# When the right factors of a matrix product are split and loaded at changes of stage

## The chip, the cores and the metric

The kernel runs on one core of a Trainium2 chip. The metric is the device time of one execution in microseconds (us); the time before is the median of three executions. A profile of one further execution shows what each engine did: TensorE (PE; its weight loads are shown as PEld), VectorE (DVE), ScalarE (ACT), GpSimd (POOL) and SyncE (SP), and the transfers (DMA) that the queues of SP, POOL and ACT issue.

## The reference

One layer of a decoder trunk over 512 tokens with 2048 channels, all in float32. The normalised input is projected into four token mixers (a gated linear recurrence, causal pooling, a short gated convolution and attention with a forget gate) and four gates per channel. Each mixer's output goes through its own branch product, is multiplied by the sigmoid of its gate, and the four are summed. Then come an output product with a residual, and an MLP of width 8192 with a squared ReLU and a residual. What the change touches is the part from the gates on:

```python
branches = jnp.einsum('bskw,kwd->bskd', ys, w_branch[l])
gates = jax.nn.sigmoid(gate_logits.reshape(b, s, N_BRANCH, d))
merged = jnp.sum(gates * branches, axis=2)
x = x + merged @ w_out[l]
h = rms_norm(x, norm_mlp_g[l]) @ w_mlp_up[l]
x = x + jnp.square(jax.nn.relu(h)) @ w_mlp_down[l]
```

## The kernel before

**Precision.** TensorE multiplies a reduced float32 form (fp32r). Each operand is split into a rounded part (names with h: `uh`, `sh`, `mgh`) and a remainder (l: `ul`, `sl`, `mgl`). ACT casts the rounded part, DVE subtracts it from the source to get the remainder, and `mm3` (L182) does three matmuls: high by high, high by low, low by high.

**Products in blocks.** Gates, MLP up and MLP down (kinds g, u and d) are computed in pairs of 128-row output tiles by a two-by-two block scheme with seven products instead of eight (`run_pair`, L923). The left factors are weights: four quarters of a 128 x 1024 raw tile (`wqg`, `wqu`, `wqd`), loaded by SP into four buffers, of which DVE forms sums (L671, into `z` tiles or in place) before they are split (`Item.cast` on ACT, L713; `Item.sub` on DVE, L719; three buffers each). The right factors are the activations: for each of eight keys a tile of seven blocks of 256 columns (the four blocks of the activation and three sums of them, made by `token_sums`, L852), split into `sh` and `sl`, 1792 columns each. A product of a pair is eight keys by three matmuls, 24 matmuls of 256 columns; a pair is 168. Seven products are evicted from PSUM by ACT copies (L936) and DVE adds (L919).

**Slots.** The split right factors lie in slots (`spools`, nine at most); `slot_of` (L865) says which key lies where. Gates and MLP up use eight fixed keys. In MLP down the keys form a sliding window over 32 tiles taken cyclically: pair n uses keys n to n+7, so from one pair to the next one new factor is needed, n+8, and it goes to a slot that the window has left. The results of MLP up are stored to device memory (`zd`) with their sums, and come back as staged tiles `std`. `bring` (L1229) does that: it issues the load of a key into a staging buffer when called (one buffer, `st1`, in the steady pairs; two at the change of stage), queues the cast `shd` (L884) and the remainder `sld` (L888), and after `sld` starts the next load into the buffer that came free.

**Changes of stage.** The last pair of one stage's products and the first of the next are done as duos (`run_duo`, L943): two pairs together in two parts, the first part with keys 0 to 3, the second with keys 4 to 7, so that some slots come free half a stage early. Between gates and MLP up lies the out stage (L1184): the merged tiles (16 slices of 128 channels, `mgh` and `mgl`) are stored to memory as they are made and loaded back in `load_merged` (L1105) into a pool that takes the place of four slots; the last two slices, 7 and 15, stay on the chip and are split there (L1131, L1132). Its last two output tiles are computed interleaved. The out results make the right factors of MLP up: factors 0 to 3 are split as they come (`in_parts`), 4 to 6 are stored and loaded back, and 7 is split at the end.

**The order of the work.** PE, ACT and DVE run in the order in which the program writes their instructions; POOL's and SP's instructions are ordered by the framework. The program runs through a list of left factors with `step` (L806): step n casts the left factor n+2, evicts the last product (`settle`, over `pending`), makes the sums for n+3 or else takes one task that waits, subtracts for n+2, writes the product's matmuls, and then takes more waiting tasks as long as an estimate of DVE's time (`busy`, advanced by `spend`) is not past an estimate of TensorE's (`clock`, advanced by `mm`). Tasks are put on the waiting list by `wait_for` (L772) with a due time on that clock. `result` (L798) forces those left by an earlier pair when a new result tile is taken, and `flush` all.

**Gates and branches.** The branch products (`bk`) were stored earlier; `next_b` (L1053) loads one back for each gate pair through POOL into a single tile `b`, after the multiply (L1070) that used the last one. **The residual** of MLP down is kept in memory (`x1d`): each pair's result is added to it by an accumulating DMA (`put`, L1298), and for the last eight pairs SP then copies the sum to the output; for the very last pair the residual is loaded, added on DVE and stored.

Of the kernel before, what the change touches and what calls it, by code (L numbers as in the profile page):

```python
# [15 lines left out]
P = 128  # L16
# [82 lines left out]
def body(nc, tc, ctx, dram):  # L99
# [672 lines left out]
    def wait_for(fn, n=0, after=0.0):  # L772

        later.append((clock[0] + after, n, fn, era[0]))

    def pop(task=None):
        task = task or later[0]
        later.remove(task)
        _, n, fn, of = task
# [13 lines left out]
    def flush(until=lambda: False):  # L793
        settle()
        while later and not until():
            pop()
# [9 lines left out]
    def step(products):  # L806
# [5 lines left out]
        settle()  # L812
        if did["sums"] <= n + 3 < len(items) and items[n + 3].sums():
# [51 lines left out]
    def slot_of(key):  # L865
# [27 lines left out]
    def in_parts(key, src, after=0.0):  # L893
        first, second = parts_of(key, src)
        wait_for(first, 0, after)
        wait_for(second, 7 * H, after)
# [26 lines left out]
    def run_pair(phase, out, u):  # L923
# [7 lines left out]
        def products(item):  # L931
            (i,) = item.group
            p = ps[at[i]]
            product(phase, i, item.left, p, i not in (2, 3), True, i in (2, 3))
            if i in (1, 2):
                return [lambda: A.copy(c11, p)]  # L936
            args = {6: (u2, p, c11), 7: (u3, p, u2), 4: (c21, p, u3), 5: (c22, p, u3), 3: (c12, p, u2)}[i]
            return [lambda: add(*args)]
# [121 lines left out]
    def merge(n, g):  # L1060
# [8 lines left out]
        def first():  # L1069
            V.tensor_tensor(out=m if k == 0 else g, in0=g, in1=b, op=ALU.mult)  # L1070
            next_b(n + 1)
# [20 lines left out]
    next_b(0)  # L1092

# [9 lines left out]
    mgpool = []  # L1103

    def load_merged():  # L1105
        closed(*(spools[j] for j in (3, 2, 1, 0)))
        mgpool.append(opened("merged", "right"))
        stage["a"] = mgpool[0][1]
        BUFS["a"] = 28
# [18 lines left out]
    for e in range(2):  # L1128
# [4 lines left out]
        mg[7 + 8 * e] = (hi, lo)  # L1133
# [11 lines left out]
    def residual(n, ps):  # L1145
# [5 lines left out]
        def first():  # L1151
# [3 lines left out]
            wait_for(scaled, S)  # L1155
            wait_for(square)

        if e == 0:
            factors[j] = wide(f"x2_{j}", *((st1, "st1", 1) if j % 2 else (opool, "o", 1)))
        o = factors[j]  # L1160
# [7 lines left out]
        def scaled():  # L1168
            V.scalar_tensor_tensor(
                out=o[:, e * S : (e + 1) * S], in0=r, scalar=pc("g_mlp", n), in1=p, op0=ALU.mult, op1=ALU.mult,  # L1170
            )
            if e:
                wait_for(sums, 4 * 300)

        def sums():
            token_sums(o)
            if j < 4:
                in_parts(("u", j), o)
            elif j < 7:
                G.dma_start(zd["u"][j], o)  # L1180
# [3 lines left out]
    for j in range(7):  # L1184
        for n in (j, j + 8):
            ps = bank(f"pw{n}")
            before = None
            for h in range(2):

                def products(item):  # L1190
# [5 lines left out]
                    for k in ks:  # L1196
                        wk = [t[:, k % 8 * P : (k % 8 + 1) * P] for t in ws[k // 8]]
                        mm3(ps, wk, mg[k], k == 0, h == 1 and k == ks[-1])
# [5 lines left out]
    for h in range(2):  # L1204

        def products(item):
            other = items[taken[0]].left
            for k in range(8):
                for (n, ps), w in zip(last.items(), (item.left, other)):
                    wk = [t[:, k * P : (k + 1) * P] for t in w]  # L1210
                    mm3(ps, wk, mg[8 * h + k], h == 0 and k == 0, h == 1 and k == 7)
            return []

        step(products)
        step(lambda item: [r for n, ps in last.items() for r in residual(n, ps)] if h else [])
    flush()
    up_scale = t512("g", "ups")
    A.copy(up_scale, ip)
    closed(mgpool[0])
    for j in range(4):  # L1220
        spools[j] = opened(f"t{j}", "right")
# [183 lines left out]
```

## Time and profile before

| | |
|---|---|
| median of three runs | 2849.2 us (2846.93 to 2855.21) |
| the profiled execution | 2849.29 us, of which the span from the first to the last instruction is 2847.5 |
| PE busy | 2738.3 us (96%), 19808 matmuls |
| DVE busy | 2167.8 us (76%) |
| ACT busy | 1230.2 us (43%) |
| memory | 151 GB/s on the mean |

Stages by the first matmul of each: gates until about 1270, out until 1457, MLP up until 2112 (its first duo until 1516, its last duo from 2072), MLP down to the end (its first duo until 2189). In the lines of the profile, out<-in names a tile and what it is made from; a bracket gives the idle time of the engine ahead of an instruction and what ended it. A row of the windows view gives a stretch, its length, each engine's busy time with its count of instructions, the clock granted to TensorE, the share of the DMA engines and GB/s.

### The profile page before, as it was taken

How to read it: one execution, taken by the hardware profiler on the slowest of the kernel's cores; microseconds unless marked ns; L12 is line 12 of the kernel's file. 1: busy time of each engine (PE TensorE's matmuls, PEld its weight loads, DVE VectorE, ACT ScalarE, POOL GpSimd, SP SyncE). 2: the span in 40 equal slices, each digit the busy share in tenths (PEclk: the TensorE clock that was granted, in tenths of full speed). 3: DMA queues.
4: the chain of work that ended last, by engine and by line, in shares of the span. 5: the costliest groups of instructions: out<-in, count | busy, mean ns of one | idle time of the engine just before them, and what ended most of it. 6: DMA issues, size and time to landing. Idle time of an engine off the chain costs nothing. (4 is left out here: it accounts for less than half of the span.)

```text
span 2847.5 us, 47968 instructions
## 1 busy us (share of the span) xinstructions
PE 2738.3 (96%) x19808; PEld 2550.9 (90%) x19808; DVE 2167.8 (76%) x2662; ACT 1230.2 (43%) x1520; POOL 179.4 (6%) x296
## 2 busy tenths in 40 slices
PE   8999999999999999999989999999977899999999
PEld 7787777789999999997879999999977899999998
DVE  6865654568888888875568988888887677777777
ACT  5443434554444444443233444444444444444443
POOL 3000000000000000021100000000000000000000
PEclk9999999999999999999999999999988999999999
DMA  5232223664444444474544444544444555555565
GB/s 181 85 97 88 78 69 128 201 217 138 147 150 155 142 155 146 145 229 152 166 144 150 160 156 151 163 143 157 162 169 158 154 147 171 172 158 162 173 192 148
DMA packets 143468, 431.31 MB, mean 151 GB/s; under 512 B 16648, under 2 KB 29576, under 8 KB 143248
## 3 DMA queue, kind: packets, MB, share of 16 engines
q1 hardware_dynamic: 101392, 279.19, 30.1%
q0 software_dynamic: 32208, 131.48, 15.6%
q10 hardware_dynamic: 9648, 17.57, 1.7%
q8 instruction: 155, 2.54, 0.4%
q14 instruction: 65, 0.53, 0.1%
HBM read 350.95 MB, written 80.89 MB: 152 GB/s over the span
## 5 line engine op out<-in xcount | busy, mean ns | idle before, releaser
L719 DVE TENSOR_TENSOR uld<-wqd,uhd 128x1024 fp32r<-128x1024 f32 (+3 forms) x136 | 157.2, 1158 | 90.9 <-ACT uhd L713 90.9
L713 ACT CAST uhg<-wqg 128x1024 fp32r<-128x1024 f32 (+1 forms) x136 | 135.5, 999 | 185.3 <-PE pgd L173 96.4
L713 ACT CAST uhu<-wqu 128x1024 fp32r<-128x1024 f32 (+1 forms) x144 | 136.3, 952 | 166.9 <-PE pud L173 88.8
L713 ACT CAST uhd<-wqd 128x1024 fp32r<-128x1024 f32 (+3 forms) x136 | 135.3, 997 | 154.5 <-PE pda L173 72.9
L151 DVE TENSOR_TENSOR wl<-wr,wh 128x1024 fp32r<-128x1024 f32 (+2 forms) x100 | 121.6, 1218 | 89.2 <-ACT wh L150 88.9
L719 DVE TENSOR_TENSOR ulg<-wqg,uhg 128x1024 fp32r<-128x1024 f32 (+1 forms) x136 | 157.1, 1157 | 33.6 <-ACT uhg L713 33.6
L150 ACT CAST wh<-wr 128x1024 fp32r<-128x1024 f32 (+2 forms) x100 | 101.1, 1014 | 159.6 <-PE pb L173 34.1
L719 DVE TENSOR_TENSOR ulu<-wqu,uhu 128x1024 fp32r<-128x1024 f32 (+1 forms) x144 | 157.7, 1100 | 13.4 <-PE pw L173 8.3
L713 ACT CAST uhg<-zg 128x1024 fp32r<-128x1024 f32 (+1 forms) x102 | 102.0, 1000 | 150.0 <-DVE ulg L719 103.3
L713 ACT CAST uhd<-zd 128x1024 fp32r<-128x1024 f32 (+3 forms) x102 | 101.8, 998 | 150.2 <-DVE zd L671 78.0
L173 PE MATMUL pda<-sld,uhd 128*128 128x256 f32 x480 | 138.2, 288 | 27.6 <-DVE sld L888 27.5
L713 ACT CAST uhu<-zu 128x1024 fp32r<-128x1024 f32 (+1 forms) x108 | 103.2, 955 | 125.4 <-DVE ulu L719 77.7
L173 PE MATMUL pdd<-shd,uhd 128*128 128x256 f32 x480 | 137.1, 286 | 3.4 <-DVE y L919 1.9
L173 PE MATMUL pda<-shd,uld 128*128 128x256 f32 x480 | 136.4, 284 | 3.8 <-DVE uld L719 3.6
L173 PE MATMUL pdd<-shd,uld 128*128 128x256 f32 x480 | 136.1, 284 | 3.5 <-DVE uld L719 3.5
L173 PE MATMUL pda<-shd,uhd 128*128 128x256 f32 x480 | 135.6, 283 | 0.4 <-ACT shd L884 0.4
L173 PE MATMUL pdd<-sld,uhd 128*128 128x256 f32 x480 | 135.6, 282 | 0.0
L173 PE MATMUL pdb<-shd,uld 128*128 128x256 f32 x480 | 134.5, 280 | 0.0
L173 PE MATMUL pdb<-sld,uhd 128*128 128x256 f32 x480 | 134.5, 280 | 0.0
L173 PE MATMUL pdb<-shd,uhd 128*128 128x256 f32 x480 | 134.4, 280 | 0.0
L173 PE MATMUL pgd<-shg,ulg 128*128 128x256 f32 x480 | 134.3, 280 | 0.0
L173 PE MATMUL pgb<-shg,ulg 128*128 128x256 f32 x480 | 134.3, 280 | 0.0
(1447 smaller groups left out, 10481.6 us busy)
## 6 DMA issues: line engine op xcount, KB each, us to landing
wqg<-in_w SPq DMA_DIRECT2D x120, 512.0 KB, 3.5
wqu<-in_w SPq DMA_DIRECT2D x112, 512.0 KB, 3.5
wr<-in_w SPq DMA_DIRECT2D x84, 512.0 KB, 3.5
std<-zd POOLq DMA_DIRECT2D x39, 896.0 KB, 6.9
zd<-h POOLq DMA_DIRECT2D x32, 896.0 KB, 4.8
bk<-b ACTq DMA_DIRECT2D x64, 256.0 KB, 2.7
b<-bk POOLq DMA_DIRECT2D x32, 512.0 KB, 4.5
wo<-in_w SPq DMA_DIRECT2D x32, 512.0 KB, 3.5
```

The costliest lines, as they stand in the source:

```text
L150: A.copy(hi, raw)
L151: V.tensor_tensor(out=lo, in0=raw, in1=f(hi), op=ALU.subtract)
L173: T.matmul(out, w, x, start=start, stop=stop, skip_group_check=more)
L713: A.copy(self.hi[:, sl], self.phase.source(i))
L719: V.tensor_tensor(out=lo, in0=self.phase.source(i), in1=f(hi), op=ALU.subtract)
```

## The change

- Waiting tasks can be marked `must`: `step` takes all of them that are due, right after the evictions and ahead of the sums and the subtraction, whatever the estimate of DVE's time; the others are taken as before.
- `bring` goes. `fetch` issues a load, `place_down` queues cast and remainder of a staged factor as `must` and then fetches a named following key into the buffer, and `renew` does this at given times. Around the change from up to down, keys 0 and 1 are loaded two pairs ahead, 0 to 3 are due at 0, 2.5, 11 and 15 from the second part of up's last duo, 4 to 7 at the same times from the start of down's first, 8 and 9 at 1 and 9 from its second part. In a steady pair n, factor n+8 is due 1.4 after the start, and factor n+9 is fetched behind it.
- The merged slices are loaded into the slots' own tiles instead of a pool in their place: six slices of 512 columns at three to a tile, and the seventh in two halves of 256 columns, for each half of the keys. `out_product` runs over these pieces. The last two output tiles are computed one after the other in each half, not interleaved. After the first half, factors 4 and 5 of MLP up are fetched; 6 and 7 are split from the tiles in which they were made.
- The branch tile `b` has two buffers, loaded two gates ahead.
- The last pair's residual is loaded ahead and added to blocks as they come; its output leaves in three stores.

```diff
-    def wait_for(fn, n=0, after=0.0):
-        later.append((clock[0] + after, n, fn, era[0]))
+    def wait_for(fn, n=0, after=0.0, must=False):
+        later.append((clock[0] + after, n, fn, era[0], must))
...
-    def next_task():
-        return next((t for t in later if t[0] <= clock[0]), None)
+    def next_task(must=False):
+        return next((t for t in later if t[0] <= clock[0] and t[4] == must), None)
...
             ensure("cast", n + 2)
             settle()
+        while t := next_task(True):
+            pop(t)
         if did["sums"] <= n + 3 < len(items) and items[n + 3].sums():
...
-        if kind == "u" or j < 8:
-            return (j + 4) % 8
-        return {8: 4, 9: 5, 10: 8}[j] if j < 11 else slot_of((kind, j - 9))
+        if kind == "u":
+            return (4, 5, 6, 7, 3, 2, 0, 1)[j]
+        return {8: 4, 9: 5, 10: 8}[j] if j in (8, 9, 10) else (j + 4) % 8 if j < 8 else slot_of((kind, j - 9))
...
+    def fetch(key, where):
+
+        t = wide(f"st{key[0]}{key[1]}", *where)
+        G.dma_start(t, zd[key[0]][key[1] % UP])
+        return t
...
-            b = wide(f"b{k}_{j}", gpool, "b", 1, 1024)
+            b = wide(f"b{k}_{j}", gpool, "b", 2, 1024)
...
-            next_b(n + 1)
+            next_b(n + 2)
...
-        closed(*(spools[j] for j in (3, 2, 1, 0)))
-        mgpool.append(opened("merged", "right"))
-        for n in (*range(7), *range(8, 15)):
-            mg[n] = [t512("a", f"mg{q}{n}", F32R) for q in "hl"]
-            for q, t in zip("hl", mg[n]):
-                G.dma_start(t, md[q, n])
+        for at, slots in ((0, (2, 3)), (8, (0, 1))):
+            room = [
+                spools[n][1].tile([P, 7 * H], F32R, name=f"mg{q}s{n}", tag=f"s{q}{n}", bufs=1)
+                for n in slots for q in "hl"
+            ]
+            for i in range(6):
+                both = []
+                for q in range(2):
+                    t, c = divmod(2 * i + q, 3)
+                    both.append(room[t][:, c * S : (c + 1) * S])
+                    G.dma_start(both[q], md["hl"[q], at + i])
+                mg[at + i] = [(slice(0, S), both)]
+            mg[at + 6] = []
+            for h in range(2):
+                sl = slice(h * H, (h + 1) * H)
+                both = [room[2 * q + h][:, 3 * S :] for q in range(2)]
+                for q in range(2):
+                    G.dma_start(both[q], md["hl"[q], at + 6][:, sl])
+                mg[at + 6].append((sl, both))
+
+    def out_product(ps, left, k, first, last):
+        wk = [t[:, k % 8 * P : (k % 8 + 1) * P] for t in left]
+        for sl, x in mg[k]:
+            mm3(ps[:, sl], wk, x, first, last)
...
+            elif j == 7:
+                in_parts(("u", 6), factors[6], 0, True)
+                in_parts(("u", 7), factors[7], 5, True)
...
+        if h == 0:
+
+            flush()
+            u4 = fetch(("u", 4), (spools[2], "sh2", 1))
+            u5 = fetch(("u", 5), (st1, "st1", 1))
+            in_parts(("u", 4), u4, 5, True)
+            in_parts(("u", 5), u5, 5, True)
...
+    def fetch_down(J):
+        if J < UP + 7:
+            staged[J] = fetch(("d", J), (upool[0], "s", 1) if J % 2 and J < 10 else ST1)
+
+    def place_down(J, after, following):
+        in_parts(("d", J), staged[J], after, True, lambda: fetch_down(following))
+
+    def renew(keys, times, following):
+        for J, t, m in zip(keys, times, following):
+            wait_for(lambda J=J, m=m: place_down(J, 0, m), 0, t, True)
...
+        if n == UP - 4:
+            fetch_down(0)
+            fetch_down(1)
...
-    brought = bring([("d", J) for J in range(10)], [ST1, ST], lambda n: 5 if n == 4 else 3)
+    TIMES = (0, 2.5, 11, 15)
...
+        lambda: renew((0, 1, 2, 3), TIMES, (2, 3, 4, 5)),
...
+    renew((4, 5, 6, 7), TIMES, (6, 7, 8, 9))
...
+        lambda: renew((8, 9), (1, 9), (10, UP + 7)),
...
         if n + 1 < UP:
-            load = bring([("d", n + 8)], [ST1], None)
-            wait_for(load, 0, 6)
-        run_pair(phase, r, u)
-        wait_for(lambda n=n, r=r: put(n, r))
+            renew((n + 8,), (1.4,), (n + 9,))
+            run_pair(phase, r, u)
+            pending.append(lambda n=n, r=r: put(n, r))
+            continue
+        x1 = wide("x1r", *ST1)[:, R]
+        G.dma_start(x1, x1d[n % 8])
...
+        run_pair(phase, r, u, {
+            7: lambda: add_in(u2, u2, x12),
+            4: lambda: add_in(c21, c21, x21),
+            5: lambda: (add_in(c22, c22, x22), out(1, slice(0, S))),
+            2: lambda: (add_in(c11, c11, x11), out(0, slice(0, H))),
+            3: lambda: out(0, slice(H, S)),
+        })
```

More of the change, by code (lines that the diff above doesn't have):

```diff
@@ L795, in flush @@
         while later and not until():
-            pop()
+            pop(min(later, key=lambda t: t[0]))
     def result(name, where, tag, cols):
@@ L891, in parts_of, with in_parts, last @@
         return first, second
-    def in_parts(key, src, after=0.0):
+    def in_parts(key, src, after=0.0, must=False, then=None):
         first, second = parts_of(key, src)
-        wait_for(first, 0, after)
-        wait_for(second, 7 * H, after)
+        def last():
+            second()
+            if then:
+                then()
+        wait_for(first, 0, after, must)
+        wait_for(last, 7 * H, after, must)
+    def fetch(key, where):
+        t = wide(f"st{key[0]}{key[1]}", *where)
+        G.dma_start(t, zd[key[0]][key[1] % UP])
+        return t
     def wide(name, where, tag, bufs, cols=7 * H):
@@ L921, in body, with run_pair @@
     turn = [0]
-    def run_pair(phase, out, u):
+    def run_pair(phase, out, u, then={}):
         tag = ("mm", "aux")[turn[0] % 2]
@@ L1154, in first @@
             G.dma_start(x1d[j][:, e * S : (e + 1) * S], r)
-            wait_for(scaled, S)
+            wait_for(scaled, S, 0, n == 15)
             wait_for(square)
-        if e == 0:
-            factors[j] = wide(f"x2_{j}", *((st1, "st1", 1) if j % 2 else (opool, "o", 1)))
-        o = factors[j]
         def square():
@@ L1168, in scaled @@
         def scaled():
+            if e == 0:
+                factors[j] = wide(f"x2_{j}", *((st1, "st1", 1) if j % 2 else (opool, "o", 1)))
+            o = factors[j]
             V.scalar_tensor_tensor(
@@ L1204, in body @@
     for h in range(2):
[L1206 to L1221, printed above, removed]
-    in_parts(("u", 7), factors[7])
-    closed(opool, ppool)
-    upool = opened("up", "left")
-    n2 = []
-    scale = chain(token_scale(acc, "r2", n2, (6, 12)))
-    def bring(keys, wheres, gap):
-        loaded = {}
-        def load(n):
-            if n < len(keys):
-                kind, j = keys[n]
-                loaded[n] = wide(f"st{kind}{j}", *wheres[n % len(wheres)])
-                G.dma_start(loaded[n], zd[kind][j % UP])
-        def parts(n):
-            if n == len(keys):
-                return
-            first, second = parts_of(keys[n], loaded[n])
-            def then():
-                second()
-                load(n + len(wheres))
-                parts(n + 1)
-            after = gap(n) if n >= len(wheres) else 0
-            wait_for(first, 0, after)
-            wait_for(then, 7 * H, after)
-        for n in range(len(wheres)):
-            load(n)
-        return lambda: parts(0)
@@ L1257, in body, with products @@
-    ST1, ST = (st1, "st1", 1), (upool, "s", 1)
-    bring([("u", 4)], [ST], None)()
-    wait_for(lambda: bring([("u", 5), ("u", 6)], [ST1, ST], None)())
+        for n, ps in last.items():
+            def products(item):
+                for k in range(8):
+                    out_product(ps, item.left, 8 * h + k, h == 0 and k == 0, h == 1 and k == 7)
+                return residual(n, ps) if h else []
+            step(products)
+        if h == 0:
[4 more added lines that the diff above has]
+            in_parts(("u", 5), u5, 5, True)
@@ L1261, in up_tiles, with begin_up @@
+    n2, upool, scale = [], [], []
+    ST1, ST = (st1, "st1", 1), None
+    def begin_up():
+        up_scale = t512("g", "ups")
+        flush()
+        A.copy(up_scale, ip)
+        closed(opool, ppool)
+        upool.append(opened("up", "left"))
+        scale.extend((chain(token_scale(acc, "r2", n2, (3, 6))), up_scale))
     def up_tiles(n):
-        return result(f"h{n}", upool, "o", 7 * H), half_wide(f"uu{n}", upool)
+        return result(f"h{n}", upool[0], "o", 7 * H), half_wide(f"uu{n}", upool[0])
```

61 lines of the change are left out of this document (29 added, 32 removed).

## The prediction

> **What bounds it now.** I read the page first, then the windows view cut at the stages, then the waits of TensorE, then the timeline of the MLP's second half.
>
> ```profile
> span 2847.5 us, 47968 instructions
> PE 2738.3 (96%) x19808; PEld 2550.9 (90%) x19808; DVE 2167.8 (76%) x2662; ACT 1230.2 (43%) x1520; POOL 179.4 (6%) x296
> PE   8999999999999999999989999999977899999999
> PEclk9999999999999999999999999999988999999999
> core 0: us, PE busy (x) PEld busy (x) DVE busy (x) ACT busy (x) POOL busy (x), PEclk, DMA share, GB/s
> 1270.47:1300.00 29.53, 25.33 (x95) 18.50 (x94) 11.71 (x14) 6.92 (x8) 5.84 (x11) 0.88 0.75 250
> 1300.00:1434.00 134.00, 134.00 (x579) 108.50 (x578) 70.27 (x88) 37.91 (x40) 14.06 (x26) 1.00 0.47 157
> 1457.43:1515.81 58.38, 47.44 (x353) 45.86 (x352) 47.28 (x81) 27.06 (x39) 2.68 (x5) 0.85 0.37 129
> 1600.00:2040.00 440.00, 440.00 (x3755) 440.00 (x3755) 390.44 (x495) 198.36 (x225) 12.22 (x23) 1.00 0.48 154
> 2092.20:2189.15 96.95, 67.32 (x502) 63.94 (x501) 72.22 (x110) 41.96 (x56) 6.74 (x12) 0.84 0.50 175
> 2189.15:2822.00 632.85, 594.12 (x4874) 582.15 (x4873) 483.46 (x497) 272.34 (x291) 40.39 (x57) 0.99 0.56 167
> ```
>
> TensorE is the bound and busy nearly everywhere, so what counts is how fast it issues. MLP up is the clean stage: 3755 matmuls in 440.00 us is 0.1172 us for a 256-wide one. A pair of 168 then needs 19.69 us, a product of 24 needs 2.81. A 512-wide one costs 134.00/579 = 0.2314. Against these rates four places lose time. The 29 pairs of MLP down (4872 matmuls) should take 571.0 and take 632.85: 61.9 lost, a pair 21.82 instead of 19.69. Up's last half and down's first two pairs (504 matmuls, 59.1) take 96.95: 37.9 lost. Up's first two pairs (336 matmuls, 39.4) take 58.38: 19.0. The first 95 matmuls of the out stage (22.0) take 29.53: 7.5. DVE is at 483.46/29 = 16.7 us a pair in down, so it does not bound there; at the change of stage its 72.22 is above TensorE's 59.1, so there it can.
>
> Why down loses 2.1 us a pair:
>
> ```profile
> PE pda L173 <- DVE sld L888: 27.5, 26, 1.7
>   DMA std<-zd: 100.8, 28
> 2392.43 2.01 DVE L888 TENSOR_TENSOR sld<-std,shd 128x1792 fp32r<-128x1792 f32 x1
> 2394.36 1.22 DVE L719 TENSOR_TENSOR uld<-wqd,uhd 128x1024 fp32r<-128x1024 f32 x1
> 2394.74 0.56 POOL L1237 DMA_DIRECT2D std<-zd  x1 [0.87 <-DVE sld L888]
> 2394.96 1.05 ACT L713 CAST uhd<-wqd 128x1024 fp32r<-128x1024 f32 x1 [2.72 <-PE pda L173]
> 2395.92 0.36 ACT L936 COPY y<-pda 128x256 f32<-128x256 f32 x1
> 2402.37 1.70 ACT L884 CAST shd<-std 128x1792 fp32r<-128x1792 f32 x1 [3.57 <-DMA std<-zd]
> 2405.04 1.23 DVE L719 TENSOR_TENSOR uld<-wqd,uhd 128x1024 fp32r<-128x1024 f32 x1 [2.79 <-ACT uhd L713]
> 2413.99 2.02 DVE L888 TENSOR_TENSOR sld<-std,shd 128x1792 fp32r<-128x1792 f32 x1
> DMA to landing us min/median/max: 4.7/6.9/8.9
> 2393.03 0.85 POOL L1301 DMA_DIRECT2D x1d<-y  x1 [19.36 <-ACT uhd L713]
> wqg<-in_w SPq DMA_DIRECT2D x120, 512.0 KB, 3.5
> ```
>
> It is a loop. One buffer (st1) stages the next right factor; its load starts when sld has read the last one (2394.74), lands near 2402.3, the cast shd stands 3.57 us at the head of ACT for it, the left casts queue behind, DVE idles 2.79, then works off its backlog without a gap until the next sld at 2413.99: 21.56 us after the last, longer than a pair's 19.69. And sld comes after the pair has begun, so TensorE waits about 1 us for it besides.
>
> **The change, part by part.**
>
> *D, the steady pairs of down.* The split of factor n+8 now falls due 1.4 into pair n in the program's clock, is taken ahead of everything else that waits, and its load was issued one pair earlier, by the step that split factor n+7. No instruction is added. The old loop opens: load after sld (8 us into a pair), landing by 16 at the median 6.9, wanted at 24. What is late next? A step casts two products ahead, and 1.4 falls due at the second step. There ACT does the left cast (0.95 to the next start), the eviction copy (0.27, if its successor too begins 0.09 early, as the copy at 2395.92 does), then shd (1.70); DVE does sld (1.93 to the next start) and only then the left remainder uld (1.22). With 0.2 for hand-overs that is 6.3 us from the step's start; its third matmul two products on wants uld after 5.62 + 0.23 = 5.85. So I expect TensorE to wait 0.5 us there. A second cost I can only bound: that later uld frees a raw buffer later, and the weight load then runs beside the factor's load; DVE reads it some 4.4 us after the release, against a landing of 3.5 (the page's median for gate weights of the same size) to 6.9 (std's, the larger transfer beside it): 0 to 2.5 late, of which DVE's 3 us of slack a pair hides most. I take 0.18. Pair: 19.69 + 0.5 + 0.18 = 20.37; 29 × (21.82 − 20.37) = **42** gained. Bounds: 61.9 (nothing waits) and 24 (a pair of 21.0, the full 1.3 of waiting).
>
> *C, up to down.*
>
> ```profile
> 2120.30 0.43 DVE L856 TENSOR_TENSOR h<-h 128x256 f32<-128x256 f32 x1 [1.12 <-ACT h L1279]
> 2115.00:2120.00 5.00, 0.00 (x0) 0.00 (x0) 4.18 (x8) 0.79 (x1) 0.00 (x0) 0.63 0.41 124
> 2120.00:2125.00 5.00, 1.37 (x3) 0.79 (x3) 4.60 (x7) 1.84 (x2) 1.06 (x2) 0.50 0.51 201
> 2130.00:2135.00 5.00, 4.84 (x29) 4.85 (x30) 2.09 (x5) 0.62 (x1) 0.53 (x1) 0.67 0.93 341
> ```
>
> Before, factors 2 and 3 are split after down has begun, and TensorE stands from 2115. Now factors 0 and 1 are loaded some pairs ahead, and 0 to 3 are split at 0, 2.5, 11 and 15 into up's last half. The same DVE work must fit into less time: 72.22 plus one more split (ten, not nine, by the end) is 74.2, so that is the floor, not 59.1. I add three waits for the squaring on ACT (1.12 each) and 4 for factor 4: its load needs the buffer that factor 2 leaves, split at the first step past 11 (11.5 in the program's clock, in which 24 matmuls are 2.56 and not 2.81: 12.6 us on the chip), read out near 17.4, so it lands near 25 while down starts at 19.7 and asks for it in its first step; the left remainder queued behind it on DVE, wanted at 25.3, comes at 29.8. Sum 81.6; gain 96.95 − 81.6 = **15**. Bounds: 21 (76, DVE never waits) and 5 (factors 5 and 7 late by as much as well, clock lost again).
>
> The Trainium skill (TensorE: Matmul & The Clock Gate, The HAM clock gate) says that about 3.4 us without work halves the matmul clock and about as long at work restores it. The rows agree: 0.50 in the stall, 0.67 in the 5 us after it. By that rule one remaining stall of 4 us costs up to 1.7 more and the sum would be 83.3 for C; cut into pieces under 3 us it would be 81.6 as taken.
>
> *A, gates to out.*
>
> ```profile
> PE pw L173 <- ACT mgh L1131: 3.8, 1, 3.8
> 1274.59 0.53 POOL L1057 DMA_DIRECT2D b<-bk  x1 [0.30 <-issue]
> 1282.70 1.22 DVE L1070 TENSOR_TENSOR g<-g,b 128x1024 f32<-128x1024 f32 x1 [10.43 <-DMA b<-bk]
> ```
>
> The last branch tile b was queued on POOL behind 28 merged loads, 10.43 us of DVE waiting. With two tiles it is loaded before them, and the merged pair 7 and 15 is ready some 9 us sooner. What is late next is the last merged load: POOL issues 32 instead of 28 (0.53 each, same bytes); the last can land near 1281.5 (b, queued one later, let DVE go at 1282.70), while TensorE wants the fourteenth slice at 1270.47 + 13 × 0.694 = 1279.5. So 2 of the 7.5 stay: gain **5.5** (3 to 7.5). Slices 6 and 14 in two 256-wide halves: 32 × (6 × 0.1172 − 3 × 0.2314) = 0.3 lost.
>
> *B, out to up.*
>
> ```profile
> 1491.49 3.98 DVE L888 TENSOR_TENSOR slu<-stu,shu 128x1792 fp32r<-128x1792 f32 x2 [4.79 <-ACT shu L884]
> 1527.25 0.37 ACT L936 COPY h<-pua 128x256 f32<-128x256 f32 x1 [4.70 <-DMA zd<-h]
> ```
>
> Factors 4 to 6 came back from memory only in up's first half and were split at its end. Now 4 and 5 are fetched into freed slots one out step (5.6 us) earlier than the stage's end, and 6 and 7 are split from where they lie, one round trip gone. TensorE's floor is 39.4 plus 1.7 for the token scale's small products, 41; the ceiling is DVE's 47.28 with some waiting, 52. Two splits (4) move in front and two stay in a first half where DVE already has its 19.7 us full, so I take 46: gain **12.5** (6 to 17). The 4.70 wait for the store of h at the first whole pair keeps its cause, at most two result tiles, and stays.
>
> *E, the end.*
>
> ```profile
> 2842.38 0.42 DVE L919 TENSOR_TENSOR y<-pdd,ud 128x256 f32<-128x256 f32 x1 [5.24 <-PE pdd L173]
> 2842.90 1.29 DVE L1143 TENSOR_TENSOR y<-y,x1r 128x512 f32<-128x512 f32 x2
> ```
>
> The residual is added block by block inside the last pair, so the 1.4 us from 2842.80 to 2844.19 leaves the tail; the extra adds lie under the last products. Gain **1.4**.
>
> Sum: 5.5 + 12.5 + 15 + 42 + 1.4 − 0.3 = 76.1. The profiled execution took 2849.29 (span 2847.5 and 1.8 around it), and the median of the runs is 2849.2, the same. 2849.3 − 76.1 = **2773**.
>
> **Rivals.** *Clear run* (2741): the forced split hides entirely, pairs at 19.69 as in up, which has DVE busier (390.44 of 440) and no stall; gains 61.9 + 21 + 17 + 7.5 + 1.4 = 108.8. Against it: in up no 1792-wide split stands before a left remainder.
>
> *Splits in the way* (2809): each forced split costs its full 1.3 a pair, and the transitions gain only at their lower ends: 24 + 5 + 6 + 3 + 1.4 = 39.4. For it: before, a late cast already idled DVE 2.79 behind ACT.
>
> *Load behind the accumulation* (2913, slower): x1d<-y and std<-zd share POOL's queue, whose order the program does not write out. If the load of a pair is queued behind that pair's x1d, it waits for the last eviction, some 20.5 into the pair, lands about 9 us into the next (20.5 + 0.85 + 0.56 + 6.9 − 19.7), and the forced cast holds ACT: the left remainder comes at 14.2 instead of 8.66, 5.5 lost each pair, 29 × (25.2 − 21.82) = 98 against 34 gained elsewhere: 64 slower. It decides once the load lands over 7 us into a pair (3.3 us lost). Against: the load waits only for sld, 12 us before that eviction. The Trainium skill (TensorE: Matmul & The Clock Gate, engine queue depths) calls the ACT and DVE queues strictly first in, first out; the 3.57 and the 2.79 behind it agree, and by that rule nothing passes the cast.
>
> **How the numbers follow.** Forecast 0.56, clear run 0.24, splits in the way 0.14, accumulation 0.04, no difference 0.02. About 0.3%, 8.5 us, is what can be told from no change; every case but the last two is beyond it: faster 0.94, same 0.02, slower 0.04. The forecast's own bounds with one part at an end are 2753 to 2791; taking in most of both neighbours, 2738 to 2811 leaves about 0.15 outside.
>
> **What would show it.** D: no idle of ACT for std in the steady pairs, std issued early in a pair, pairs of 20.2 to 20.5 us with a short TensorE wait on uld at the fourth product; 19.7 is the clear run, 21 the splits. C: 2092 to down's third pair in about 82 us, DVE busy over nine tenths, a cast waiting on factor 4. A: no wait on b, a short one on the last merged slice. B: 46 us for up's first two pairs, the wait for h's store still there. I am wrong if the pair does not drop below 21, or if the transitions gain nothing because DVE's queue only moves its backlog.

## The result, and the profile after

The changed kernel takes 2806.8 us (median; 2804.96 to 2810.41) where the kernel before took 2849.9 (2846.93 to 2855.21) on the same chip: ratio 0.9848, 95% interval 0.983 to 0.9866. It is faster by 43 us. The prediction had the sign and 2806.8 lies in its range, near the upper end; it forecast 76 us, so a little over half of the gain came. The range holds it only because it was drawn to take in the neighbouring rivals; the forecast's own bounds, 2753 to 2791, do not. The profiled execution has a span of 2805.6 us against 2847.5, 41.9 less.

The page of the changed kernel, in the lines that answer to those of before (the span; busy time and share of each engine; TensorE's busy tenths and granted clock in forty slices):

```profile
span 2805.6 us, 48202 instructions
PE 2722.6 (97%) x19904; PEld 2547.5 (91%) x19904; DVE 2162.5 (77%) x2664; ACT 1229.7 (44%) x1520; POOL 180.4 (6%) x298
PE   8999999999999999999999999999997999999999
PEclk9999999999999999999999999999998999999999
```

A slice is some 70 us. Of the two dips before, that at out to up (one slice) no longer shows, and that at up to down (three slices) is down to one. The loss at gates to out was too short to show as a dip. The windows view of the changed kernel, cut at the first matmul of each stage (stretch, length, busy time of PE, PEld, DVE, ACT and POOL with counts, granted clock, share of the DMA engines, GB/s): out; up's first two pairs; up's last half and down's first two pairs; down's first whole pair; its other 28 pairs; the end from the last pair on.

```profile
1272.20:1452.60 180.40, 180.07 (x866) 148.84 (x865) 93.94 (x118) 52.01 (x57) 23.50 (x44) 1.00 0.52 173
1452.60:1502.68 50.08, 43.68 (x353) 43.04 (x352) 44.58 (x78) 23.84 (x38) 0.54 (x1) 0.97 0.27 90
...
2078.01:2167.43 89.42, 67.15 (x506) 64.14 (x505) 74.02 (x112) 41.78 (x55) 6.75 (x12) 0.90 0.56 190
2167.43:2196.25 28.82, 22.84 (x170) 22.46 (x169) 20.18 (x21) 10.42 (x11) 1.42 (x2) 0.88 0.44 127
2196.25:2782.30 586.05, 561.24 (x4707) 556.34 (x4705) 458.11 (x476) 262.45 (x280) 39.45 (x56) 1.00 0.59 175
2782.30:2805.59 23.29, 20.00 (x170) 19.79 (x168) 11.25 (x16) 5.89 (x7) 0.85 (x1) 1.00 0.29 68
```

So a pair of the 28 went from 21.79 us to 20.93, not to 20.37, and the first whole pair, 22.84 before, became 6.0 longer. By the terms of the prediction (us; the last three columns are gains, the last one that of e7, the best variant of the experiments):

| term | length before | after | predicted | changed kernel | e7 |
|---|---|---|---|---|---|
| before out, not touched | | | 0 | -1.7 | -1.1 |
| A, out stage | 186.96 | 180.40 | 5.2 | 6.6 | 7.6 |
| B, up's first two pairs | 58.38 | 50.08 | 12.5 | 8.3 | 8.3 |
| up's 28 pairs | 556.17 | 555.61 | 0 | 0.6 | 0.8 |
| C, up's last half, down's first two pairs | 97.46 | 89.43 | 15 | 8.0 | 15.3 |
| D, 29 pairs of down | 632.85 | 614.86 | 42 | 18.0 | 57.4 |
| E, the end | 25.51 | 23.29 | 1.4 | 2.2 | 2.2 |
| sum | | | 76.1 | 41.9 | 90.6 |

The first half of up's last two pairs, 19.72 in each kernel, is left out. The first row is scatter: the out stage begins between 1270.19 and 1272.20 in the profiles of all variants, which are alike up to there.

**Gates to out.** DVE's multiply by the last branch tile, then the one wait of TensorE from 1265 to 1300:

```profile
1275.13 1.23 DVE L1085 TENSOR_TENSOR g<-g,b 128x1024 f32<-128x1024 f32 x1 [1.12 <-ACT g L1088]
```

```profile
PE pw L173 <- DMA mgls<-mdl: 0.3, 2, 0.2
```

The 10.43 us for `b` are gone, and the last merged slices hardly delay TensorE.

**Down's pairs.** First the waits of TensorE from 2190 to 2790 in the changed kernel (waiter and line, what it waited for, us in total, times, longest), then its timeline in one pair, whose first product starts at 2468.44 and whose second, number 6, at 2471.27 (start, duration, engine, line, operation; in the bracket the idle time ahead and what ended it):

```profile
PE pdb L173 <- DVE ud L933: 24.8, 28, 0.9
```

```profile
2474.34 2.02 DVE L890 TENSOR_TENSOR sld<-std,shd 128x1792 fp32r<-128x1792 f32 x1 [3.47 <-ACT shd L886]
2476.28 1.22 DVE L719 TENSOR_TENSOR uld<-wqd,uhd 128x1024 fp32r<-128x1024 f32 x1
2477.42 0.42 DVE L933 TENSOR_TENSOR ud<-pdb,y 128x256 f32<-128x256 f32 x1
...
2471.40 1.05 ACT L713 CAST uhd<-wqd 128x1024 fp32r<-128x1024 f32 x1 [1.78 <-PE pda L173]
2472.35 0.36 ACT L951 COPY y<-pda 128x256 f32<-128x256 f32 x1
2472.61 1.70 ACT L886 CAST shd<-std 128x1792 fp32r<-128x1792 f32 x1
...
2476.67 0.56 POOL L909 DMA_DIRECT2D std<-zd  x1 [6.25 <-DVE sld L890]
```

The loop of before is open: the load `std` starts 8.2 us into the pair before the one that casts it, and the cast `shd` waits for no transfer. The new wait is where the prediction put one, at the fourth product, and it is longer and for something else. DVE stands 3.47 us for the cast, does `sld`, then the left remainder `uld`, and only then the addition that reads product 6 out of bank b, into which product 4 is to go. The fourth product starts 1.06 us late in every pair (3.88 us after the third in the median, where 2.82 would do; the row's 0.9 is less because it counts from the end of a matmul, which lasts 0.28 us while the next starts 0.12 after it). The prediction had 0.5, for the remainder.

**The first whole pair.** The timeline again, DVE and POOL:

```profile
2171.42 1.22 DVE L719 TENSOR_TENSOR uld<-wqd,uhd 128x1024 fp32r<-128x1024 f32 x1
2178.69 2.03 DVE L890 TENSOR_TENSOR sld<-std,shd 128x1792 fp32r<-128x1792 f32 x1 [6.06 <-DMA x1d<-y]
...
2171.80 0.87 POOL L1325 DMA_DIRECT2D x1d<-y  x1 [15.90 <-DVE y L933]
```

Slot 8 is opened over the pool that held up's results and down's first two. The forced split into it waits until the accumulating store of the second result has been read out (issued 2171.80), and DVE, 6.06 us idle, holds everything behind it.

**Up to down.** Waits of DVE, then of TensorE, from 2078 to 2168:

```profile
DVE sld L890 <- ACT shd L886: 8.9, 7, 2.3
DVE ud L933 <- ACT y L979: 3.5, 2, 2.4
...
PE pd L173 <- DVE uld L719: 11.0, 7, 3.9
PE pu L173 <- DVE ulu L719: 6.0, 4, 2.9
PE pd L173 <- ACT shd L886: 2.7, 1, 2.7
PE pd L173 <- DVE sld L890: 1.5, 1, 1.5
```

DVE is busy 74.02 us in the stretch (the prediction's 74.2), yet it also idles 8.9 in front of its splits, whose casts come just ahead of them on ACT, while left remainders stand behind. The last two rows are one right factor that came late (7, by its place in the order).

**Out to up.** DVE's splits, then two rows about the store of `h` in the first whole pair:

```profile
1453.59 2.03 DVE L890 TENSOR_TENSOR slu<-stu,shu 128x1792 fp32r<-128x1792 f32 x1 [1.76 <-ACT shu L886]
1460.75 2.02 DVE L890 TENSOR_TENSOR slu<-x,shu 128x1792 fp32r<-128x1792 f32 x1
1468.18 2.02 DVE L890 TENSOR_TENSOR slu<-x,shu 128x1792 fp32r<-128x1792 f32 x1 [1.67 <-ACT shu L886]
...
1513.83 0.37 ACT L951 COPY h<-pua 128x256 f32<-128x256 f32 x1 [5.74 <-PE puc L173]
1514.01 0.54 POOL L909 DMA_DIRECT2D std<-zd  x1 [4.10 <-DMA zd<-h]
```

The stage begins at 1452.60, so of the two splits that were to move ahead of it one ends 3 us inside. The bracket of the copy names TensorE, but the copy starts as the store of `h` lands (issued at 1509.37, landed at 1513.73). The stage cut after its first 20 us:

```profile
1452.60:1472.60 20.00, 13.60 (x96) 12.96 (x95) 17.09 (x23) 8.62 (x12) 0.54 (x1) 0.91 0.20 66
1472.60:1502.68 30.08, 30.08 (x259) 30.07 (x258) 27.48 (x57) 15.22 (x27) 0.00 (x0) 1.00 0.32 106
```

TensorE loses its time in the first 20 us, where DVE is busy for 17.09 of them, and has no gap after that.

### The profile page after: what moved, and what is told of

The parts are those of the page before. It is cut to its first block, busy times and chain, and to the rows that moved or that the text cites. A ratio compares the mean times of both kernels' runs of the same rounds, so it can differ in the third digit from the quotient of the medians.

```text
span 2805.6 us, 48202 instructions
## 1 busy us (share of the span) xinstructions
PE 2722.6 (97%) x19904; PEld 2547.5 (91%) x19904; DVE 2162.5 (77%) x2664; ACT 1229.7 (44%) x1520; POOL 180.4 (6%) x298
## 5 line engine op out<-in xcount | busy, mean ns | idle before, releaser
L890 DVE TENSOR_TENSOR sld<-std,shd 128x1792 fp32r<-128x1792 f32 x39 | 78.9, 2025 | 111.9 <-ACT shd L886 105.8
```

The lines of the kernel that those rows point to most:

```text
L890: V.tensor_tensor(out=lo, in0=src, in1=f(hi), op=ALU.subtract)
```

## The experiments

All are versions of the changed kernel except the last. Ratios are to the kernel before on the same chip.

**Is it the eviction of bank b, or DVE's throughput?** Four variants of the steady pairs. e1 moves the split's due time:

```diff
-            renew((n + 8,), (1.4,), (n + 9,))
+            renew((n + 8,), (4.0,), (n + 9,))
```

> The changed kernel with one number changed: in the steady pairs of MLP down the split of the next right factor falls due 4.0 into the pair in the program's clock instead of 1.4, that is after the step that evicts product 6. Nothing is left out. Theory EVICTION: the pair takes 20.93 us and not 19.69 because product 4 wants bank b, and the addition that empties bank b stands on VectorE behind the forced split and the left remainder (TensorE waited 30.0 us in all for it, 29 times). With the split behind that addition the wait goes: pairs of 19.7 to 19.9 us, the wait of TensorE for that addition below 5 us in all, the run 28 to 35 us shorter, about 2775. Theory THROUGHPUT (VectorE and ScalarE simply need the 20.9 us with this order, wherever the split is put): pairs stay within 0.2 of 20.93 and the run within 6 us. Theory NEXT IN LINE: the wait moves to the left remainder or to the eviction of the next product, pairs near 20.3 to 20.4, the run 14 to 18 us shorter.

Measured: 2782.1 us, ratio 0.9749 (0.9721 to 0.9777). The 28 pairs:

```profile
2189.72:2755.17 565.45, 565.08 (x4707) 558.09 (x4706) 457.90 (x477) 265.66 (x280) 39.46 (x56) 1.00 0.63 181
```

20.19 a pair, and no wait on the addition. The same DVE and ACT work fits into less, so throughput is out. The pair stays 0.3 above the 19.7 to 19.9 of the eviction theory, and the run is 24.7 us shorter, not 28 to 35: the last three products take 3.01, 2.93 and 2.91 us instead of 2.83, with no wait recorded. What these are wasn't settled.

e2 gives product 4 the unused half of the same bank:

```diff
-        ps = {c: bank(f"p{phase.kind}{c}", tag)[:, :H] for c in "abcd"}
-        at = {1: "a", 2: "a", 6: "b", 4: "b", 7: "c", 5: "d", 3: "d"}
+        ps = {c: bank(f"p{phase.kind}{c}", tag) for c in "abcd"}
+        ps = {**{c: p[:, :H] for c, p in ps.items()}, "e": ps["b"][:, H:]}
+        at = {1: "a", 2: "a", 6: "b", 4: "e", 7: "c", 5: "d", 3: "d"}
```

> The changed kernel with product 4 of each pair written to the unused second half of bank b's 512 columns instead of the first half, so that it needn't wait for the addition that reads product 6; queues and order stay as they are. Nothing is left out. Theory EVICTION (the last waiter at product 4 is the bank): the wait of TensorE at product 4 falls from 1.06 us a pair to what the left remainder still costs, by the prediction 0.5 us, and the pair from 20.93 to 20.3 to 20.5; the run 12 to 18 us shorter, about 2792. If the left remainder is in time, the pair comes to 19.7 to 19.9 and the run to about 2775. Theory REMAINDER (the left remainder alone is late and the bank is ready anyway): pair 20.93 unchanged, run within 4 us.

Measured: 2805.9 us, ratio 0.9834 (0.9805 to 0.9864), pairs 20.93, TensorE's waits in down:

```profile
PE pdb L173 <- DVE ud L933: 24.8, 28, 0.9
```

The same row: the program's dependence covers the whole bank, so the edit took no wait away and decides nothing. The Trainium skill (PSUM — Partial Sum Buffer, PSUM bank collisions raise a hardware error) says why it should: two engines in one bank at once collide even in disjoint columns. No run here shows a collision, only the wait.

e2b exchanges banks. The order of the products is 1, 6, 7, 4, 5, 2, 3, so two products (7 and 4) now lie between product 6 and the next in bank b, where it was one (7). Between products 5 and 3, which share a bank in both, there is still one:

```diff
-        at = {1: "a", 2: "a", 6: "b", 4: "b", 7: "c", 5: "d", 3: "d"}
+        at = {1: "a", 2: "a", 6: "b", 4: "d", 7: "c", 5: "b", 3: "b"}
```

> The changed kernel with two PSUM banks exchanged: product 4 goes to bank d, products 5 and 3 to bank b, in all pairs and half pairs, so that no product follows into a bank less than three products after the one whose sum must be read out of it. The forced split stays ahead of everything, as in the changed kernel. Nothing is left out. The variant with the second half of bank b gave pairs of 20.94 with the same wait for the same addition (24.8 us, 28 times): the program holds the whole bank, so it did not take the wait away. Theory EVICTION: now product 4 waits for the left remainder at most; by the prediction's reckoning 0.5 us, pair 20.2 to 20.4, the run 15 to 21 us shorter than the changed kernel's 2806.8; if the remainder is in time, 19.7 to 19.9 and 30 us. Theory REMAINDER (the left remainder is as late as the bank): pair above 20.7, the run within 6 us.

Measured: 2785.6 us, ratio 0.9754 (0.9739 to 0.9768). The 28 pairs, and what TensorE waits for in them:

```profile
2191.24:2759.60 568.36, 562.08 (x4706) 556.37 (x4705) 455.63 (x476) 262.57 (x280) 39.46 (x56) 1.00 0.62 180
```

```profile
PE pdd L173 <- DVE uld L719: 6.3, 28, 0.2
```

20.30 a pair. With the order untouched and only the bank freed, what is left is a wait for the left remainder: the fourth product starts on time, stands at its third matmul and takes 3.32 us, 0.50 more than 2.82. That is the prediction's own mechanism and size. The eviction is shown to cost the rest, 0.63 of the pair's 20.93.

e3a takes the forced split behind the step's left remainder, in the steady pairs alone:

```diff
         settle()
-        while t := next_task(True):
+        while not late[0] and (t := next_task(True)):
             pop(t)
...
         ensure("sub", n + 2)
+        while t := next_task(True):
+            pop(t)
...
     dpool = opened("down", "left")
+    late[0] = True
```

> The changed kernel, but from the steady pairs of MLP down on the forced split is taken behind the step's left remainder instead of ahead of it; it is still ahead of the eviction of product 6. Nothing is left out. Theory EVICTION: the left remainder comes 1.9 us sooner, the cast of it is no longer behind the split's cast, and the addition that empties bank b stands behind one thing less that waits; the pair comes to 19.7 to 20.2 and the run 20 to 35 us shorter. Theory THROUGHPUT: pair 20.93 as before, the run within 6 us. The opposite is possible too: if the addition of product 6 still stands behind remainder and split, the order of the two doesn't matter to it and the pair stays at 20.7 to 20.9.

Measured: 2773.7 us, ratio 0.9717 (0.9682 to 0.9752). Windows view of the 28 pairs, and DVE's timeline at the start of one:

```profile
2195.46:2750.30 554.84, 554.82 (x4706) 554.56 (x4705) 460.18 (x476) 262.65 (x280) 39.46 (x56) 1.00 0.63 185
```

```profile
2457.04 1.23 DVE L719 TENSOR_TENSOR uld<-wqd,uhd 128x1024 fp32r<-128x1024 f32 x1 [1.61 <-ACT uhd L713]
2458.90 2.02 DVE L894 TENSOR_TENSOR sld<-std,shd 128x1792 fp32r<-128x1792 f32 x1 [0.64 <-ACT shd L890]
2460.84 0.42 DVE L937 TENSOR_TENSOR ud<-pdb,y 128x256 f32<-128x256 f32 x1
```

19.82 a pair, against TensorE's 19.69, and no wait of TensorE. DVE fills the time of the cast with the remainder, waits 0.64 instead of 3.47, and the addition ends in time though it still stands behind both. So the 0.50 and the 0.63 are both the price of the split's place in two queues that run in order, not of the split. The 0.12 that stay over 19.69 are spread over the pair: 2.83 us for every product, 2.81 in up.

**The first whole pair: slot 8?** e4 makes only that pair's split due at 13:

```diff
-            renew((n + 8,), (1.4,), (n + 9,))
+            renew((n + 8,), (13 if n == 2 else 1.4,), (n + 9,))
```

> The changed kernel with the split of the first whole pair of MLP down (factor 10, into slot 8) due at 13 in the program's clock instead of 1.4; all other pairs as they are. Nothing is left out. Theory SLOT 8: the first whole pair takes 28.82 us because this split writes memory over which the result tile of down's second pair lay, and that tile is free only when its accumulating store has landed (VectorE stood 6.06 us for it). Put behind it, the split doesn't stand: the pair takes 20.5 to 22 us, the run is 6 to 8 us shorter, about 2800, steady pairs 20.93 unchanged. Theory FACTOR LATE (another of the factors 6 to 9, or TensorE's slower clock, keeps the pair long): the pair stays above 27 and the run within 2 us.

Measured: 2804.1 us, ratio 0.9826 (0.9797 to 0.9854). The first pair and the second, and the second's cast:

```profile
2168.00:2188.69 20.69, 19.94 (x170) 19.74 (x169) 16.02 (x18) 10.26 (x11) 0.87 (x1) 1.00 0.47 128
2188.69:2214.57 25.88, 21.89 (x171) 21.50 (x169) 20.73 (x20) 9.63 (x11) 1.97 (x3) 0.93 0.58 177
```

```profile
2196.26 1.69 ACT L886 CAST shd<-std 128x1792 fp32r<-128x1792 f32 x1 [1.69 <-DMA std<-zd]
```

The first pair becomes 8.1 us shorter, as theory SLOT 8 has it, and the second 4.9 longer: the one staging buffer comes free later and the next factor with it. The run was 2.7 us shorter and not 6 to 8; I had looked at one pair and not at what its load feeds.

**Up to down: order, or DVE as the floor?** e3b is e3a, but from up's last two half pairs on (the flag `late` set earlier).

> The changed kernel with the forced split behind the step's left remainder, not ahead of it, from up's last two half pairs on (the variant before did so from the steady pairs of down on, and gave pairs of 19.81). Nothing is left out. From the start of up's last half pairs to the end of down's first whole pair the changed kernel took 137.96 us, of them 46.56 in up's last half, 62.58 in down's first, 28.82 in the first whole pair. Theory ORDER (splits in front hold the remainders back, VectorE idles for casts): up's last half 40 to 43, down's first half 50 to 58, 8 to 16 us in all besides the first whole pair. Theory VECTOR BOUND (VectorE's work at the change of stage is the floor, the order only moves the waits): the three together within 4 us of 137.96, steady pairs 19.81, the run about 2774.

Measured: 2766.7 us, ratio 0.9684 (0.9668 to 0.97). Up's last half and down's first pairs, then the first whole pair:

```profile
2076.82:2159.14 82.32, 67.13 (x506) 64.40 (x505) 73.18 (x111) 41.62 (x55) 6.74 (x12) 0.92 0.64 207
2159.14:2188.26 29.12, 23.13 (x168) 22.75 (x169) 20.32 (x22) 10.41 (x11) 1.42 (x2) 0.88 0.43 126
```

82.32 for 89.42: order is worth 7.1 us, just short of the 8 that its theory gave as the least (up's last two half pairs took 43.30, down's first 58.73). DVE's waits for the casts of splits fall from 8.9 us to 0.4. It now idles 9 us of 82, so it is near the floor.

e7 sets the flag in `begin_up` and puts 8 in place of 13 for the first whole pair. It does less than its text expects: `begin_up` runs between the two parts of up's first pairs, after a `flush` that has emptied the waiting list, so all four splits of that stage have been written by then.

> The changed kernel with two things: the forced split behind the step's left remainder from the beginning of MLP up on (so in up's first half pairs, in up's last, and in all of down), and the split of the first whole pair of down due at 8 in the program's clock instead of 1.4. Nothing is left out. Steady pairs 19.81. Up's first half pairs took 50.08 us in the changed kernel: by theory ORDER they take 45 to 47, by VECTOR BOUND 49 to 51. The first whole pair took 28.82 and the second 20.97; put at 13, they took 20.69 and 25.88 (the buffer came free too late for the next factor). By theory SLOT 8, at 8 they take 20 to 22 and 19.8 to 20.5. The run: 2755 to 2763 by both theories that gain, 2774 if neither gains, beneath the variant that moved the split only in the steady pairs (2773.7) by 11 to 19 us.

Measured: 2759.5 us, ratio 0.9662 (0.9648 to 0.9677), and e8, e9, f1 and f2 below lie within 1 us of it:

```profile
1450.87:1500.97 50.10, 43.68 (x353) 43.04 (x352) 44.56 (x78) 23.83 (x38) 0.54 (x1) 0.97 0.27 90
2076.05:2158.25 82.20, 67.27 (x506) 64.86 (x504) 73.18 (x111) 41.62 (x55) 6.75 (x12) 0.92 0.64 207
2158.25:2179.17 20.92, 20.09 (x169) 19.88 (x169) 19.07 (x21) 10.54 (x11) 1.42 (x2) 1.00 0.55 155
2179.17:2733.66 554.49, 554.49 (x4706) 554.49 (x4705) 460.07 (x477) 262.72 (x280) 39.44 (x56) 1.00 0.64 186
```

The first whole pair is 20.92 and the second 19.87, so both slot 8 and the feedback of e4 hold. Up's first pairs stay at 50.10, but that tests nothing: from 1445 on, DVE's and ACT's instructions in them stand in the same order as in the changed kernel. Theory ORDER was not tried in this stage.

**Out to up: what holds it?** e8 is e7 with factors 4 and 5 due at once (`in_parts(("u", 4), u4, 0, True)` and the same for 5, instead of 5).

> The variant with the split behind the remainder from up on and the first whole pair's split at 8, and with the splits of factors 4 and 5 of MLP up due at once when their loads are issued in the last out steps, not 5 later in the program's clock. Nothing is left out. In that variant and in the changed kernel alike up's first half pairs took 50.1 us, whatever the order; ScalarE cast factor 4 at 1446.3 in it (1448.09 in the changed kernel), some 2.5 us after its load had landed, and VectorE had idled 3.85 and 1.88 us just before. Theory SPLITS TOO LATE (the two splits that were to move ahead of up still end 3 us into it): they end 2 to 3 us sooner, and up's first half pairs take 47 to 48.5. Theory FOUR SPLITS (all four splits, the scalings and the remainders of the first half together are too much for VectorE's time there): within 1 us of 50.1. The run within 3 us of 2759.5 or 1.5 to 3 us under it.

Measured: 2759.8 us, ratio 0.9673 (0.9659 to 0.9686). DVE's splits:

```profile
1445.05 2.03 DVE L894 TENSOR_TENSOR slu<-stu,shu 128x1792 fp32r<-128x1792 f32 x1 [9.14 <-ACT shu L890]
1448.84 2.02 DVE L894 TENSOR_TENSOR slu<-stu,shu 128x1792 fp32r<-128x1792 f32 x1 [1.76 <-ACT shu L890]
```

Both splits have now ended by 1450.86, 0.8 us after up starts (1450.05), and up's first pairs take 50.90: no gain. The first cast waited 3.29 us for its load at the head of ACT, and the left casts that came 5.6 us ahead of up's start in the changed kernel (1447.04) came 1.5 after it (1451.55). f1 and f2 are e7 with factors 6 and 7 due at 4 and 8, and at 8 and 12, instead of 0 and 5.

> The variant with the split behind the remainder from up on (2759.5 us, up's first half pairs 50.10), with the splits of factors 6 and 7 of MLP up due at 4 and 8 in the program's clock instead of 0 and 5. Nothing is left out. They are wanted only by the second part of up's first half pairs, some 20 us on, while in the first part TensorE waits for left remainders three times, 6 us in all, the longest 3.8, at a time when the split of factor 6 stands ahead of them on VectorE. Theory SPLIT IN FRONT (part B was lost to this order): the longest wait loses the 2.0 us of the split, up's first half pairs take 47 to 48.5 and the run 2 to 3 us less. Theory FULL QUEUE (VectorE has the whole work of that part to do in any order): within 0.7 us of 50.10, the wait comes later.

> As the variant with 4 and 8, but the splits of factors 6 and 7 of MLP up due at 8 and 12. Nothing is left out. Theory SPLIT IN FRONT: 45.5 to 48, at or below the variant with 4 and 8, since both splits then stand behind the first part's remainders. Theory FULL QUEUE: 49.4 to 50.8. Should the second part then wait for factor 7, above 51.

Measured: 2759.0 (ratio 0.9669, 0.9655 to 0.9683) and 2760.4 (0.9676, 0.9662 to 0.9689), up's first pairs 50.17 and 51.14. TensorE's waits from 1445 to 1525 in f1 show that the wait is not gone:

```profile
PE pu L173 <- DVE ulu L719: 7.2, 4, 2.9
```

The longest wait did fall, from 3.8 us to 2.9, but the sum rose from 6.4 to 7.2. The split of factor 6 went to a later step, where it again stood ahead of that step's remainder, and DVE waited for its cast (7.4 us for the casts of the four splits in f1, 5.3 in the changed kernel). So a later due time gains nothing here. f1 fits FULL QUEUE; f2's 51.14 lies above both theories, and TensorE has no recorded wait for factor 7 in it.

What holds up's first pairs at 50 stays open. In the changed kernel DVE is busy 44.58 of the 50.08 us and stands 3.4 more for the casts of splits and 1.7 for those of remainders, so with the same work in the stage at most 5.5 us can be gained. But no run took work away from DVE here, and none put the splits of this stage behind the step's left remainder, the move that gained 7.1 us at up to down.

e9 is e8 with the banks of e2b.

> The variant with factors 4 and 5 split at once, and the banks of product 4 and products 5 and 3 exchanged besides. Nothing is left out. With the split behind the remainder no wait of TensorE in down's pairs was left to see (pairs 19.81, TensorE's floor 19.69). If the eviction of product 6 still costs the 0.12, the pairs come to 19.7 and the run 3 us lower; if not, pairs 19.81 and no difference in the steady pairs. At the change of stage from up to down (102 us for up's last and down's first half pairs) a freer bank could gain 1 to 4 us where VectorE's additions are late, or nothing if the remainders and splits are what is late.

Measured: 2759.3 us, ratio 0.967 (0.9657 to 0.9683); pairs 19.81, up to down 82.09. With the split behind, the exchange of banks gains nothing; the last 0.12 a pair is not the wait for the eviction.

**Part A alone.** b1 is the kernel before with

```diff
-            b = wide(f"b{k}_{j}", gpool, "b", 1, 1024)
+            b = wide(f"b{k}_{j}", gpool, "b", 2, 1024)
...
-            next_b(n + 1)
+            next_b(n + 2)
```

and a second `next_b` at the start.

> The kernel before with one part of the change alone: two tiles for the branch products b, the second loaded one product ahead; the merged loads still go to a pool of their own and the right factors come as before. Nothing is left out. By the prediction's part A the wait of VectorE for b (10.43 us) goes, and the out stage, 186.96 us, takes 181 to 182.5 us, the run 4 to 6 us shorter; nothing else changes. By the rival that the merged slices laid into the slots are what gains, it stays within 2 us of 186.96.

Measured: 2846.7 us, ratio 0.9976 (0.9961 to 0.9992). The out stage:

```profile
1270.51:1451.80 181.29, 180.01 (x770) 143.88 (x769) 91.15 (x117) 49.09 (x55) 21.00 (x39) 1.00 0.51 167
```

5.7 us shorter in the out stage, of the 6.6 of the whole change; by the interval the run is 2 to 11 shorter. The second tile of `b` is nearly all of part A.

## Why the prediction was right or wrong

**D, 42 forecast, 18.0 measured: the failed step is the sum of 0.95, 0.27, 1.70, 1.93, 1.22 and 0.2 for hand-overs, set against 5.85.** It followed the left remainder to its end and stopped there. The instruction behind it on DVE was left out: the addition that frees bank b for the same fourth product. The fourth product started 1.06 late, not 0.5. e2b shows the difference to be the bank: without it the product stands 0.50 and the pair is 20.30 against the forecast's 20.37. That the pair comes so near is in part luck, for the 0.18 for late weight loads is not in the trace: between 2200 and 2740 ACT stood nine times for such loads, 22.7 us in all, and TensorE waited for nothing but the addition. In its place stand the 0.12 spread over all products. The other part of the miss is the first whole pair, 6.0 longer than before and counted at 20.37: the prediction didn't ask what lies under the slot into which the forced split writes. The pair of 20.93 is only just under the 21 above which the prediction was to count as wrong. 28 × (20.93 − 20.37) = 15.7 and 28.82 − 20.37 = 8.5 make the 24 that are missing. That the old loop opens, that the load starts early, and that ACT no longer waits for it were right; the load behind the accumulation did not happen.

**C, 15 forecast, 8.0 measured.** The floor by DVE's work was right (74.2 forecast, 74.02 busy). The failed steps are the waits added to it. The term for factor 4 (4 us) is not in the trace: no cast waited for a load there. Its load landed 24.5 us into up's last half (2102.52), as forecast, but that half took 26.85 us and not 19.7, so it was in time. Of the three waits for the squaring one came (1.1). In their place DVE idled 8.9 us before splits whose casts had only just been queued. With remainders in front (e7) the same stretch takes 82.20, against 81.6 forecast, but by another sum: 0.4 for those casts and 6.6 for two additions that waited for a copy on ACT. So the time was reachable, but not with the order that the change wrote. On the clock, three rows of e7 (the windows view in stretches of 5 us) show what waits of 0.8, 2.1 and 3.7 us close behind each other do:

```profile
2120.00:2125.00 5.00, 1.59 (x9) 0.98 (x8) 4.90 (x9) 4.02 (x5) 0.60 (x2) 1.00 0.39 97
2125.00:2130.00 5.00, 1.82 (x8) 1.82 (x9) 3.13 (x3) 0.00 (x0) 0.99 (x2) 0.56 1.01 387
2130.00:2135.00 5.00, 5.00 (x35) 5.00 (x34) 2.68 (x4) 2.75 (x4) 0.00 (x0) 0.76 0.66 199
```

35 matmuls in the third row where 45 stand in the next one: 1.2 us lost after 6.6 of waiting in the two before. The rule of the Trainium skill (TensorE: Matmul & The Clock Gate, the HAM clock gate), half clock after a few idle microseconds and about as long to come back, agrees with 0.56, 0.76 and then 1.00.

**B, 12.5 forecast, 8.3 measured.** The step "two splits move in front" did not come about: one ended 3 us inside the stage. But e8 moved it all but in front and gained nothing, so that is not what cost the 4 us. TensorE lost them in the first 20 us, waiting 6.4 for left remainders, while DVE was busy for 17.09; the 46 was a choice between floor and ceiling, not a sum. Whether DVE's work or its order holds it there stays open. The wait for the store of `h` stayed, as said. The first whole pair of up took 23.41, 3.7 above TensorE's 19.69, but of its recorded waits only 0.8 us stand behind that copy and 1.7 are for left remainders.

**A and E** were right to 1.4 and 0.8 us; in A the wait of 2 for the last merged slice did not come (0.3 in all).

**The rivals.** *Splits in the way* gave 2809 and pairs of 21.0, nearest to what was measured, but by another sum: its full 1.3 of remainder is, by e2b, 0.50 of remainder and 0.63 of bank, and A, B and C all came out above its lower ends, D below its 24. *Clear run*'s pairs of 19.69 came within 0.13 once the split stood behind the remainder. That e3a's 2773.7 is the forecast's figure is chance: it gains 51 in D and 6.6 in C.

## What to carry to other kernels

A task that is forced ahead in an in-order queue must be costed against everything behind it up to the next thing the bound engine asks for, the read-out of a PSUM bank as well as the next operand. Put a long piece of work behind the short urgent one, where the wait for its first half (here ACT's cast) is filled. And for any step moved earlier, ask what memory it writes and whose last reader, a store included, must land first.

## What was not expected

The accumulating store of one result tile (128 x 1024) held the memory under it from its issue at 2171.80 to 2178.6, 6.8 us, where the 31 such stores land after 5.2 in the median; a store that nothing waits for elsewhere gave DVE its longest idle at this change of stage. And the same DVE work, 458 to 460 us in 28 pairs, went with pairs of 20.93, 20.19 and 19.82 by its order alone.
